# Where the split of the next weight chunk stands at the end of a sublayer: inside the second tile's layer norm, or ahead of the first tile's transposes

## The chip, the cores and the metric

The kernel runs on one core of one Trainium2 chip. The metric is device time in microseconds (us), of which the median over several runs counts.

## What is computed

Four post-norm layers over 256 frames of width 1024. Each layer has a token mixer (`lru` in layers 0 and 3, `rwkv` in layer 1, `attn` in layer 2), a cross-attention into 256 memory tokens (`cross`) and a squared-ReLU MLP (`mlp`): twelve sublayers, and each ends in a residual and a layer norm.

```python
for i in range(DEPTH):                       # 4
    y = mixer[i % 3](h)                      # lru, rwkv, attn
    h = _layer_norm(DEEPNORM_ALPHA * h + y, ln_g[i, 0], ln_b[i, 0])
    y = memory_cross_attention(h, mem, mx_w_q[i], mx_w_kv[i], mx_w_o[i])
    h = _layer_norm(DEEPNORM_ALPHA * h + y, ln_g[i, 1], ln_b[i, 1])
    y = squared_relu_mlp(h, mlp_w1[i], mlp_w2[i])
    h = _layer_norm(DEEPNORM_ALPHA * h + y, ln_g[i, 2], ln_b[i, 2])
```

## The kernel before

The 256 frames are two tiles of 128 rows, `h[0]` and `h[1]` (`h_91` and `h_92` in the lists of instructions below). Nothing is scheduled at run time: each engine executes its instructions in the order in which the program issues them, and that order is written by hand.

**Weights.** Class `Stream` brings all weights as a fixed sequence of chunks of 128 x 1024 f32. `_dma` issues a chunk's transfer on SP's queue into one of four `wraw` buffers. `_split` turns a landed chunk into a high part `whi` (a cast on ScalarE, ACT, line 455) and a low part `wlo` (a subtraction on VectorE, DVE, line 456), in one of seven pairs of buffers, and then issues the transfer of a later chunk. A product of two f32 matrices is three matmuls on TensorE (PE): `whi` with the high part of the other operand (line 273), `wlo` with it (274), `whi` with the low part (275). `done(c)` says that chunk c's last matmul has been issued, and splits on while buffers are free; `more()` splits one chunk more, into the pair of the chunk that was done last. Such a cast has to wait until PE has read that pair for the last time.

**The end of a sublayer.** The output projection runs tile 0, then tile 1 (`out_gemm`, in `mlp` its last block). After a tile's matmuls `resid` (lines 375, 380) adds them to `h` and takes the statistics, and `ln` (lines 387 to 401) is the layer norm: the small operations of lines 387 and 389, a power on GpSimd (POOL, line 390), two instructions of line 395 that need the mean alone, and two of line 401 that need POOL's result. `ln` calls `aside` between the power and line 395.

**The start of the next.** `next_ht` gives a function that transposes tile 0 of the new `h`: eight transposes on PE (line 352) into two PSUM tiles `tp`, out of which ACT casts the high part (line 355) and DVE subtracts the low part (line 356), both into `ht`. `mm_piece` calls it as `near` just before the last two rows' worth of weights of tile 1, so that PE has three matmuls to run behind the transposes:

```python
for k in range(kpc):
    if near and ci == n - 1 and k == kpc - 1:
        near()
```

The next sublayer's first product then runs tile 0, and the transposes of tile 1 stand in the same way ahead of its last three matmuls. Where the next sublayer is `rwkv`, `near` copies the transposed tile to `hf` (line 1134) and takes a shifted difference `xx` (line 1135) instead.

There are eleven such passages from one sublayer to the next. By what stands on DVE there, the ten that the diff touches are of four kinds: five ends of `out_gemm` with four chunks (every `cross`, and `attn`), two with six chunks in two parts (`lru`), two ends of `mlp` ahead of `attn` and `lru`, and one end of `mlp` ahead of `rwkv`. The end of `rwkv` keeps its order.

Of the kernel before, what the change touches and what calls it, by code (L numbers as in the profile page):

```python
# [29 lines left out]
G0 = 1  # L30
RES = 8
RESL = 2, 2, 2, 2
ASIDE = 1
LF = 18
LV = 0
GNP = 1
# [192 lines left out]
def _hl(hi, lo, p=128):  # L229
    return lambda kt: (hi[:p, kt, :], lo[:p, kt, :])  # L230


class Kern:
# [430 lines left out]
    def out_gemm(self, name, idx, n, lhs, p):  # L664

        for nh in range(2):
            a = [self.acc(), self.acc()]
            parts = [range(n)] if n <= 4 else [range(n // 2), range(n // 2, n)]
            for part in parts:
                end = part is parts[-1]  # L670
                ch = [self.st.take(name, (*idx, nh, q), p, 1024) for q in part]
                last = end and nh == 1
                near = self.next_ht() if last else None
                for t in range(2):
                    self.mm_piece(a[t], ch, lhs[t], p, 512, kt0=2 * part[0], start=part[0] == 0, stop=end,
                                  last=t == 1 and not last, near=near if t else None)
                    if last and t == 0:
                        self.st.more()
                    if end:
                        self.resid(t, nh, a[t])  # L680
                    if last:
                        self.ln_end(t, ch)

    def ln_end(self, t, ch):

        def aside():
            self.st.done(ch[0])
            self.st.more()

        self.ln(t, aside=aside if t and ASIDE else None)  # L690
        if t and not ASIDE:
            aside()
        if t:
            keep = DEFER if self.si < len(self.subs) and self.subs[self.si][0] != "rwkv" else 0
            for c in ch[1:len(ch) - keep]:
                self.st.done(c)
            self.owed = ch[len(ch) - keep:]
        if self.si >= len(self.subs):
            self.nc.sync.dma_start(self.out[t * 128:(t + 1) * 128, :], self.h[t])
        elif t:  # L700
            self.gb_due = 2
# [14 lines left out]
    def mlp(self, l):  # L716
        nc, tc = self.nc, self.tc
        NB = 8
        with tc.tile_pool(name="mlp", bufs=2, reuse_waits="tile") as p:
            accs = None  # L720
            sq, aT = [], {}

            def w1(b):
                hi = p.tile([128, 4, T], F32R, name="ahi", tag="ahi")
                lo = p.tile([128, 4, T], F32R, name="alo", tag="alo")
                ts = [slice(t * 128, (t + 1) * 128) for t in range(2)]
                for t in range(2):
                    aT[b, t] = _hl(hi[:, :, ts[t]], lo[:, :, ts[t]])
                if b:
                    for c, a, a2 in self.gemm_t("w1", (l, b), self.hT, (self.acc, self.acc) if b == 1 else (self.mm, self.tp)):  # L730
                        if c % 2 == 0:
                            r = p.tile([128, 2, T], F32, name="rel", tag="rel")
                        nc.scalar.copy(r[:, c % 2, :], a2)  # L733
                        nc.vector.tensor_tensor(out=r[:, c % 2, :], in0=a, in1=r[:, c % 2, :], op=ALU.add)  # L734
                        if c % 2:
                            sl = slice(c - 1, c + 1)
                            nc.vector.scalar_tensor_tensor(out=r, in0=r, scalar=0.0, in1=r, op0=ALU.max, op1=ALU.mult)  # L737
                            nc.scalar.copy(hi[:, sl, :], r)  # L738
                            nc.vector.tensor_tensor(out=lo[:, sl, :], in0=r, in1=hi[:, sl, :].bitcast(F32), op=ALU.subtract)
                            while sq:  # L740
                                self.to_hl(*sq.pop(0), 4)
                    return
                ch = self.chunks("w1", (l, b), 4, 128, 1024)
                for t in range(2):
                    a = self.mm()
                    self.mm_piece(a, ch, self.hT[t], 128, 512, last=t == 1, near=None if t else lambda: self.hT[1])
                    r = p.tile([128, 512], F32, name="rel", tag="rel")
                    nc.scalar.activation(r, a, AF.Relu)
                    nc.vector.tensor_tensor(out=r, in0=r, in1=r, op=ALU.mult)
                    sq.append((r, hi[:, :, ts[t]], lo[:, :, ts[t]]))  # L750

            for b in range(NB + 1):
                if b < NB:
                    w1(b)
                if b == 0:
                    continue
                if b == 1:
                    accs = [[self.acc() for _ in range(2)] for _ in range(2)]
                chs = [self.chunks("w2", (l, b - 1, nh), 2, 128, 1024) for nh in range(2)]
                near = self.next_ht() if b == NB else None  # L760
                for t in range(2):
                    for nh in range(2):
                        self.mm_piece(accs[t][nh], chs[nh], aT[b - 1, t], 128, 512, start=b == 1, stop=b == NB,
                                      last=t == 1 and b < NB, near=near if t and nh else None)
                        if b == NB:
                            if t == 0 and nh == 0:
                                self.st.more()
                            self.resid(t, nh, accs[t][nh])
                    if b == NB:
                        self.ln_end(t, chs[0] + chs[1])  # L770
                if b == 5 and self.coming("rwkv"):
                    self.rw_first()
# [365 lines left out]
    def rwkv(self, l, j):  # L1138
# [550 lines left out]
        oT, acc, ch = {}, [[None, None], [None, None]], [[], []]  # L1689
# [45 lines left out]
        self.mm_piece(acc[0][1], ch[1][3:], oT[0], 128, 512, kt0=6, start=False)  # L1735
        self.resid(0, 1, acc[0][1])
        near = self.next_ht()
        self.ln_end(0, ch[1])
        self.mm_piece(acc[1][1], ch[1], oT[1], 128, 512, near=near)
        self.resid(1, 1, acc[1][1])  # L1740
        self.ln_end(1, ch[1])
        r2.close()
        r1.close()
        return []
# [198 lines left out]
```

## Time and profile before

| | us |
|---|---|
| median of 3 runs | 1813.78 |
| lowest and highest of them | 1811.99, 1815.51 |
| profiled execution, its own time | 1802.43 |
| its span in the trace | 1800.6 |

The rows below are of the profiled execution. A time in them is counted from the start of the span. A DVE or ACT row merged as "x2" gives the first start and the time over both.

### The profile page before, as it was taken

To read this page: it belongs to the slowest core of one execution; us is meant where nothing else is said; L and a number is where in the kernel's file an instruction comes from. 1 tells how busy PE (TensorE), PEld (TensorE's weight loads), DVE (VectorE), ACT (ScalarE), POOL (GpSimd) and SP (SyncE) were. 2 spreads that over 40 slices of the span, in tenths; PEclk is the share of its full clock that TensorE was granted. 3 is DMA by queue.
4 is the path that set the end of the run, shared out by engine and by line. 5 is a ranking of instruction groups with operands and counts; after the bars stand their busy time and mean duration, and the time that the engine had idled before them with its cause. 6 is when DMAs were issued, how large, how long until landed. Compare 5 with 4: busy or idle time off the path is not lost.

```text
span 1800.6 us, 25667 instructions
## 1 busy us (share of the span) xinstructions
PE 1736.4 (96%) x10032; PEld 1453.8 (81%) x10032; DVE 1252.3 (70%) x1809; ACT 871.6 (48%) x1338; POOL 55.3 (3%) x64
## 2 busy tenths in 40 slices
PE   8999999999999989999999999999999999999998
PEld 7888988888777656888887888888888887988886
DVE  6587776667578798776667567776667587677665
ACT  6754534444543134544444544634444674545442
POOL 2000000000000001000000000000000000000000
PEclk9999999999999999999999999999999999999999
DMA  7464555555242224455555623545555545636552
GB/s 243 138 205 175 186 185 192 187 187 202 95 144 86 91 93 137 151 187 194 189 190 197 244 94 119 186 164 187 187 188 189 168 147 164 208 120 231 186 187 94
DMA packets 92927, 302.39 MB, mean 168 GB/s; under 512 B 11906, under 2 KB 19586, under 8 KB 92676
## 3 DMA queue, kind: packets, MB, share of 16 engines
q1 hardware_dynamic: 91780, 297.92, 49.3%
q10 hardware_dynamic: 1024, 2.81, 0.5%
q8 instruction: 79, 1.29, 0.3%
q14 instruction: 44, 0.36, 0.1%
HBM read 299.65 MB, written 1.05 MB: 167 GB/s over the span
## 4 chain that ended last, share of the span: by engine, by line
PE 78%; DVE 11%; ACT 4%; DMA 4%; issue 2%; POOL 0%; SPq 0%; DVEq 0%; ACTq 0%
PE acc L275 12%; PE acc L273 12%; PE acc L274 12%; PE tp L294 5%; PE mm L294 5%; PE acc L314 4%; PE acc L294 4%; PE acc L517 4%; PE tp L295 3%; PE mm L295 3%; DVE wlo L456 2%; PE acc L192 2%; PE mm L842 2%; PE tp L352 2%; PE acc L295 2%
## 5 line engine op out<-in xcount | busy, mean ns | idle before, releaser
L456 DVE TENSOR_TENSOR wlo<-wraw,whi 128x1024 fp32r<-128x1024 f32 (+3 forms) x505 | 593.7, 1206 | 133.3 <-ACT whi L455 121.9
L455 ACT CAST whi<-wraw 128x1024 fp32r<-128x1024 f32 (+3 forms) x505 | 507.2, 1039 | 163.5 <-PE acc L275 97.3
L273 PE MATMUL acc<-whi,ahi 128*128 128x512 f32 x512 | 200.3, 391 | 0.0
L275 PE MATMUL acc<-whi,alo 128*128 128x512 f32 x512 | 199.7, 390 | 0.0
L274 PE MATMUL acc<-wlo,ahi 128*128 128x512 f32 x512 | 199.4, 389 | 0.0
L273 PE MATMUL acc<-whi,ht 128*128 128x448 f32 (+1 forms) x368 | 142.4, 387 | 5.5 <-ACT whi L455 5.5
L274 PE MATMUL acc<-wlo,ht 128*128 128x448 f32 (+1 forms) x368 | 140.6, 382 | 3.5 <-DVE wlo L456 3.5
L275 PE MATMUL acc<-whi,ht 128*128 128x448 f32 (+1 forms) x368 | 140.4, 381 | 0.0
L294 PE MATMUL tp<-ht,whi 128*128 128x512 f32 x384 | 136.7, 398 | 0.0
L294 PE MATMUL mm<-ht,whi 128*128 128x512 f32 x384 | 136.5, 398 | 0.0
L294 PE MATMUL acc<-ht,whi 128*128 128x512 f32 x352 | 126.0, 400 | 1.9 <-DVE qkT L987 1.9
L275 PEld LDWEIGHTS acc<-whi,alo 128*128 128x128 f32 x512 | 96.1, 188 | 20.9
L273 PEld LDWEIGHTS acc<-whi,ahi 128*128 128x128 f32 x512 | 96.1, 188 | 20.2
L274 PEld LDWEIGHTS acc<-wlo,ahi 128*128 128x128 f32 x512 | 96.2, 188 | 19.2
L295 PE MATMUL tp<-ht,wlo 128*128 128x256 f32 x384 | 107.9, 281 | 0.0
L295 PE MATMUL mm<-ht,wlo 128*128 128x256 f32 x384 | 107.8, 281 | 0.0
L295 PE MATMUL acc<-ht,wlo 128*128 128x256 f32 x352 | 98.7, 280 | 0.0
L734 DVE TENSOR_TENSOR rel<-mm,rel 128x256 f32<-128x256 f32 x48 | 18.6, 425 | 110.4 <-ACT rel L733 110.4
L355 ACT CAST ht<-tp 128x512 fp32r<-128x512 f32 x40 | 22.8, 589 | 135.3 <-PE tp L352 134.3
L738 ACT CAST ahi<-rel 128x512 fp32r<-128x512 f32 x56 | 34.8, 622 | 110.0 <-DVE rel L737 110.0
L294 PEld LDWEIGHTS tp<-ht,whi 128*128 128x128 f32 x384 | 72.2, 188 | 18.0
L294 PEld LDWEIGHTS mm<-ht,whi 128*128 128x128 f32 x384 | 72.1, 188 | 17.6
(387 smaller groups left out, 3419.3 us busy)
## 6 DMA issues: line engine op xcount, KB each, us to landing
wraw<-in_w SPq DMA_DIRECT2D x256, 512.0 KB, 4.5
wraw<-in_w_kv SPq DMA_DIRECT2D x64, 512.0 KB, 4.3
wraw<-in_lru_in SPq DMA_DIRECT2D x47, 448.0 KB, 4.7
wraw<-in_w_q SPq DMA_DIRECT2D x32, 512.0 KB, 4.3
wraw<-in_w_co SPq DMA_DIRECT2D x32, 512.0 KB, 4.7
wraw<-in_ca_qkv SPq DMA_DIRECT2D x24, 512.0 KB, 4.5
wraw<-in_lru_out SPq DMA_DIRECT2D x24, 448.0 KB, 5.0
ln_gt<-in_ln_g SPq DMA_DIRECT2D x12, 512.0 KB, 6.1
```

What stands on the lines that cost most here:

```text
L192: return f(*a, **k)
L273: nc.tensor.matmul(acc[:, :w], lhsT=a, rhs=wh[:p, ws], start=s, stop=False)
L274: nc.tensor.matmul(acc[:, :w], lhsT=a, rhs=wl[:p, ws], start=False, stop=False)
L275: nc.tensor.matmul(acc[:, :w], lhsT=b, rhs=wh[:p, ws], start=False, stop=e)
L294: self.nc.tensor.matmul(four, lhsT=wh[:, ws], rhs=xy, start=s, stop=False)
L295: self.nc.tensor.matmul(four[:, :2], lhsT=wl[:, ws], rhs=x, start=False, stop=e)
L314: self.nc.tensor.matmul(a, lhsT=w[:, ws], rhs=v, start=s and i == 0, stop=e and i == 2)
L352: self.nc.tensor.transpose(dst_ps[:n, j * p:(j + 1) * p], s, self.ident[:p, :p])
L455: self.nc.scalar.copy(hi, src)
L456: self.nc.vector.tensor_tensor(out=lo, in0=src, in1=hi.bitcast(F32), op=ALU.subtract)
L517: nc.tensor.matmul(a, lhsT=u, rhs=w[:, ws], start=s, stop=e)
L842: nc.tensor.matmul(ps[:CT, gate * T:(gate + 1) * T], lhsT=gw[gate][:, n, :], rhs=xc[g][:, k, :], start=n == ks[0][0], stop=n == ks[-1][0])
```

## The change

At the ten ends, `done(ch[0])` and `more()` are called by `room`, ahead of `near`, and no longer by `aside` within the layer norm of tile 1. Each such call splits one chunk. The last layer norm of the kernel has no chunk left to split, before and after.

```diff
-                near = self.next_ht() if last else None
+                near = self.room(ch, self.next_ht()) if last else None
...
-    def ln_end(self, t, ch):
+    def room(self, ch, near):
+
+        def f():
+            self.st.done(ch[0])
+            self.st.more()
+            near()
+        return near and f
+
+    def ln_end(self, t, ch, roomy=True):
 
         def aside():
             self.st.done(ch[0])
             self.st.more()
 
-        self.ln(t, aside=aside if t and ASIDE else None)
-        if t and not ASIDE:
-            aside()
+        self.ln(t, aside=aside if t and not roomy else None)
...
-                near = self.next_ht() if b == NB else None
+                near = self.room(chs[0], self.next_ht()) if b == NB else None
...
-        self.ln_end(0, ch[1])
+        self.ln_end(0, ch[1], False)
...
-        self.ln_end(1, ch[1])
+        self.ln_end(1, ch[1], False)
```

The order of PE's, POOL's and SP's instructions stays as it is. In the changed kernel the lines behind the removed constant have a number lower by one (`wlo` is line 455, `whi` 454).

On DVE, at the end of layer 0's `cross` ahead of `mlp`: `wlo` is the split, `ht<-tp,ht` the low part of tile 0's transposes, `h_92` tile 1. Before:

```order
L401 SCALAR_TENSOR_TENSOR h_91<-h_91,rstd,ln_bt 128x512 x2
L356 TENSOR_TENSOR ht<-tp,ht 128x512 x2
L375 SCALAR_TENSOR_TENSOR h_92<-h_92,acc 128x512
L380 BN_STATS bnst<-h_92 128x6
L387 BN_AGGR bnmv<-bnst 128x2
L389 TENSOR_SCALAR rstd<-bnmv 128x1
L456 TENSOR_TENSOR wlo<-wraw,whi 128x1024
L395 SCALAR_TENSOR_TENSOR h_92<-h_92,bnmv,ln_gt 128x512 x2
L401 SCALAR_TENSOR_TENSOR h_92<-h_92,rstd,ln_bt 128x512 x2
```

After:

```order
L400 SCALAR_TENSOR_TENSOR h_91<-h_91,rstd,ln_bt 128x512 x2
L455 TENSOR_TENSOR wlo<-wraw,whi 128x1024
L355 TENSOR_TENSOR ht<-tp,ht 128x512 x2
L374 SCALAR_TENSOR_TENSOR h_92<-h_92,acc 128x512
L379 BN_STATS bnst<-h_92 128x6
L386 BN_AGGR bnmv<-bnst 128x2
L388 TENSOR_SCALAR rstd<-bnmv 128x1
L394 SCALAR_TENSOR_TENSOR h_92<-h_92,bnmv,ln_gt 128x512 x2
L400 SCALAR_TENSOR_TENSOR h_92<-h_92,rstd,ln_bt 128x512 x2
```

The split has moved from between `rstd` and the first scaling of `h_92` to between the last scaling of `h_91` and the subtraction for tile 0's `ht`. All else keeps its order.

On ACT, at the same place, `whi` is the cast of the split, `ht` the casts of tile 0 and then of tile 1. Before:

```order
L355 CAST P_2047<-mm 128x2x2x128 x2
L455 CAST whi<-wraw 128x1024 x5
L355 CAST ht<-tp 128x512 x2
L455 CAST whi<-wraw 128x1024 x2
L355 CAST ht<-tp 128x512 x2
L455 CAST whi<-wraw 128x1024
```

After:

```order
L354 CAST P_2047<-mm 128x2x2x128 x2
L454 CAST whi<-wraw 128x1024 x6
L354 CAST ht<-tp 128x512 x2
L454 CAST whi<-wraw 128x1024
L354 CAST ht<-tp 128x512 x2
L454 CAST whi<-wraw 128x1024
```

One cast has moved from behind tile 0's `ht` to ahead of it.

On DVE, at the end of layer 1's `mlp` ahead of `attn`. Before:

```order
L401 SCALAR_TENSOR_TENSOR h_91<-h_91,rstd,ln_bt 128x512 x2
L375 SCALAR_TENSOR_TENSOR h_92<-h_92,acc 128x512
L380 BN_STATS bnst<-h_92 128x6
L356 TENSOR_TENSOR ht<-tp,ht 128x512 x2
L375 SCALAR_TENSOR_TENSOR h_92<-h_92,acc 128x512
L380 BN_STATS bnst<-h_92 128x6
L387 BN_AGGR bnmv<-bnst 128x2
L389 TENSOR_SCALAR rstd<-bnmv 128x1
L456 TENSOR_TENSOR wlo<-wraw,whi 128x1024
L395 SCALAR_TENSOR_TENSOR h_92<-h_92,bnmv,ln_gt 128x512 x2
```

After:

```order
L400 SCALAR_TENSOR_TENSOR h_91<-h_91,rstd,ln_bt 128x512 x2
L374 SCALAR_TENSOR_TENSOR h_92<-h_92,acc 128x512
L379 BN_STATS bnst<-h_92 128x6
L455 TENSOR_TENSOR wlo<-wraw,whi 128x1024
L355 TENSOR_TENSOR ht<-tp,ht 128x512 x2
L374 SCALAR_TENSOR_TENSOR h_92<-h_92,acc 128x512
L379 BN_STATS bnst<-h_92 128x6
L386 BN_AGGR bnmv<-bnst 128x2
L388 TENSOR_SCALAR rstd<-bnmv 128x1
L394 SCALAR_TENSOR_TENSOR h_92<-h_92,bnmv,ln_gt 128x512 x2
```

Here the residual of half of tile 1 (`h_92`, `bnst`) stands ahead of tile 0's `ht` in both, and the split now comes between them.

## Rows read from the trace of the kernel before

**Rows 1.** The page: busy us, share of the span and instructions of each engine.
```profile
PE 1736.4 (96%) x10032; PEld 1453.8 (81%) x10032; DVE 1252.3 (70%) x1809; ACT 871.6 (48%) x1338; POOL 55.3 (3%) x64
```

**Rows 2.** Waits of PE over the span: us in total, times, longest.
```profile
PE tp L352 <- DVE h L401: 9.7, 10, 1.3
```

**Rows 3.** Timeline, DVE, `cross` to `mlp`, layer 0: start us, us, instruction [idle before].
```profile
245.04 1.41 DVE L401 SCALAR_TENSOR_TENSOR h<-h,rstd,ln_bt 128x512 f32<-128x512 f32 x2
...
247.78 1.29 DVE L356 TENSOR_TENSOR ht<-tp,ht 128x512 fp32r<-128x512 f32 x2 [1.32 <-ACT ht L355]
...
250.66 0.15 DVE L389 TENSOR_SCALAR rstd<-bnmv 128x1 f32<-128x1 f32 x1
250.74 1.23 DVE L456 TENSOR_TENSOR wlo<-wraw,whi 128x1024 fp32r<-128x1024 f32 x1
...
253.21 1.41 DVE L401 SCALAR_TENSOR_TENSOR h<-h,rstd,ln_bt 128x512 f32<-128x512 f32 x2
...
255.68 1.28 DVE L356 TENSOR_TENSOR ht<-tp,ht 128x512 fp32r<-128x512 f32 x2
```

**Rows 4.** Timeline, ACT, same end.
```profile
247.16 1.08 ACT L355 CAST ht<-tp 128x512 fp32r<-128x512 f32 x2 [8.85 <-PE tp L352]
```

**Rows 5.** Timeline, PE, same end, and layer 3's end of `cross`.
```profile
242.89 0.39 PE L275 MATMUL acc<-whi,ol 128*128 128x512 f32 x1
...
246.52 1.03 PE L352 MATMUL tp<-ident,h 128*128 128x128 f32 x8
...
254.10 1.29 PE L352 MATMUL tp<-ident,h 128*128 128x128 f32 x8 [0.96 <-DVE h L401]
...
256.41 0.50 PE L275 MATMUL mm<-whi,ht 128*128 128x512 f32 x1
...
1617.22 1.29 PE L352 MATMUL tp<-ident,h 128*128 128x128 f32 x8 [0.97 <-DVE h L401]
```

**Rows 6.** Instructions on tile `wraw` at the same end, 230 to 250 us.
```profile
L106 SPq DMA_DIRECT2D wraw<-in_w x5: 327/328/328, 233.6 to 239.9; - x5
...
DMA to landing us min/median/max: 4.6/4.8/5.0
```

**Rows 7.** Timeline, DVE then PE, `lru` to `cross`, layer 0.
```profile
150.85 1.41 DVE L401 SCALAR_TENSOR_TENSOR h<-h,rstd,ln_bt 128x512 f32<-128x512 f32 x2
...
152.98 1.40 DVE L356 TENSOR_TENSOR ht<-tp,ht 128x512 fp32r<-128x512 f32 x2 [0.72 <-ACT ht L355]
...
154.03 0.39 PE L275 MATMUL acc<-whi,ht 128*128 128x512 f32 x1
...
159.37 1.29 PE L352 MATMUL tp<-ident,h 128*128 128x128 f32 x8 [0.86 <-issue]
```

**Rows 8.** Timeline, DVE then PE, `mlp` to `attn`, layer 1.
```profile
954.25 1.29 DVE L356 TENSOR_TENSOR ht<-tp,ht 128x512 fp32r<-128x512 f32 x2
...
959.70 1.41 DVE L401 SCALAR_TENSOR_TENSOR h<-h,rstd,ln_bt 128x512 f32<-128x512 f32 x2
...
955.04 0.46 PE L275 MATMUL acc<-whi,ht 128*128 128x512 f32 x1
...
960.58 1.29 PE L352 MATMUL tp<-ident,h 128*128 128x128 f32 x8 [0.97 <-DVE h L401]
```

**Rows 9.** Timeline, DVE, `mlp` to `rwkv`; last row: chain that ended last.
```profile
428.72 0.70 DVE L380 BATCH_NORM_STATS2 bnst<-h 128x6 f32<-128x512 f32 x1
429.91 1.23 DVE L1135 TENSOR_TENSOR xx<-hf 128x1024 f32<-128x1024 f32 x1 [0.49 <-ACT hf L1134]
...
431.68 1.79 PE tp L1181 x16
```

**Rows 10.** Timeline, DVE, last layer norm of the kernel.
```profile
1794.08 0.15 DVE L389 TENSOR_SCALAR rstd<-bnmv 128x1 f32<-128x1 f32 x1
...
1795.47 1.41 DVE L401 SCALAR_TENSOR_TENSOR h<-h,rstd,ln_bt 128x512 f32<-128x512 f32 x2
```

**Rows 11.** Busy us of PE, PEld, DVE, ACT, POOL in a stretch inside `mlp`.
```profile
300.00:400.00 100.00, 100.00 (x504) 84.59 (x503) 62.85 (x73) 46.03 (x61) 0.00 (x0) 1.00 0.57 197
```

More of the change, by code (lines that the diff above doesn't have):

```diff
@@ L32 @@
 RESL = 2, 2, 2, 2
-ASIDE = 1
 LF = 18
```

## The prediction

> **What bounds the kernel.** I began with the page: PE is busy for 96% of the span [rows 1], so only what makes PE wait, or frees it from a wait, can move the end. I then read PE's waits. Their largest entry is this change's place: the transposes of tile 1 wait for line 401, the last operation of that tile's layer norm, 10 times and 9.7 us in all [rows 2]. One of the ten is the end of `rwkv`, which is not edited; the `lru` end of layer 0 has the same wait under the name "issue" [rows 7]. Last I went through DVE, ACT and PE in order of time at each of the ten edited ends, to see whether DVE has room where the split goes.
>
> At a `cross` end DVE works through tile 0's `ht`, tile 1's residual, the statistics, `rstd`, then the split (`wlo`), then lines 395 and 401, and PE stands still for 0.96 us until the first of line 401 is done [rows 3, 5]. The split lies on the chain that PE waits for. Ahead of tile 0's `ht`, in contrast, DVE idles for 1.32 us, because it needs PE's transposes and ACT's cast first [rows 3].
>
> **What taking it out of the layer norm gives.** From the start of `rstd` to the start of line 401 it is 253.21 - 250.66 = 2.55 us with the split between [rows 3]. The last layer norm of the kernel has none and takes 1795.47 - 1794.08 = 1.39 us [rows 10]; the changed order on DVE is that of this layer norm. So line 401 comes 2.55 - 1.39 = 1.16 us earlier after `rstd`. POOL's power, which runs at the same time, is in both figures. The same instruction on DVE costs as much wherever it is put; what decides is whether it fills idle time there.
>
> **Five ends with four chunks (`cross`, `attn`).** Line 401 of tile 0 ends at 245.04 + 1.41 = 246.45, and `ht` starts at 247.78 [rows 3]. The split takes 1.23 us [rows 3], so it ends near 247.7 and just fits. That needs the cast on ACT done by 246.45. ACT idles for 8.85 us up to 247.16 [rows 4], so it is free. The cast needs the chunk's transfer: five are issued between 233.6 and 239.9 and land some 4.8 us later, at most 5.0 [rows 6]; even the last of them, a later chunk, is there by 244.9. It also needs PE to be done with chunk `ch[0]`, whose last matmul for tile 1 closes the second of eight groups of three; it ends at 242.89 + 0.39 = 243.28 [rows 5]. The cast should run from about 243.4 to 244.5, and both halves of the split are hidden, the one by ACT's idle time and the other by DVE's. If the cover were missing, this end would look like those of `mlp` below.
>
> Line 401 then starts at 253.21 - 1.16 = 252.05, and what released the transposes at 254.10 does so at 252.94. PE is ready at about 254.10 - 0.96 = 253.14, so its wait is gone. Behind the transposes PE needs tile 1's low part of `ht`, which DVE started at 255.68, behind another split that follows line 401 without a pause, and the matmul with it started at 256.41 [rows 3, 5]. This is again DVE's chain, 1.16 us earlier. I take 1.16 for each of the five. The lower bound is nothing (if the split does not fit). The upper one is 0.96 plus the 0.26 that the eight transposes lose because the second line 401 comes late (1.29 us here, against 1.03 for tile 0's, which wait for nothing [rows 5]), about 1.2. Layer 3 has the same wait, 0.97 [rows 5], and so have the three between. Sum: 5 x 1.16 = 5.8 us.
>
> **Two ends of `lru`.** The gap ahead of `ht` is only 0.72 us here [rows 7]. One split occupies DVE for 1.15 us, from its start at 250.74 until the next instruction could start; I get it as 2.55 - 1.39, rounded. It starts as line 401 ends, 152.2, and `ht` starts near 153.32 instead of 152.98: 0.34 late. From the start of `ht` to the first matmul with a low part it is 0.79 us where PE waits for it (954.25 to 955.04 [rows 8]), so that matmul comes at 154.11 instead of 154.03 [rows 7]: PE loses 0.08. Tile 1's line 401 comes 1.16 - 0.34 = 0.82 earlier, and PE, which waited 0.86 for it [rows 7], follows by as much. 0.8 us each, between 0 and 0.86. Sum: 1.6 us.
>
> **Two ends of `mlp` ahead of `attn` and `lru`.** Here tile 0's `ht` starts on DVE at 954.25 with no idle time before it [rows 8]: half of tile 1's residual and statistics already fill the gap. The split in front delays `ht` by 1.15, and the matmul at 955.04, which waits for it, with it [rows 8]. The rest of DVE's chain is the same work in another order, so line 401 stays near 959.70, and the transposes near 960.58: PE's wait of 0.97 there [rows 8] turns into a wait of 1.15 at the low part. I count 0, between a loss of 0.2 and a gain of 0.3 each.
>
> **One end of `mlp` ahead of `rwkv`.** DVE idles 0.49 us ahead of `xx` [rows 9]. With the split there from 429.4, `xx` ends near 431.7 instead of 429.91 + 1.23 = 431.14, and PE's matmuls on it start at 431.68 [rows 9]. I count a loss of 0.1, at most 0.3. PE does not wait for line 401 here.
>
> **Queues.** SP's queue keeps its order; a transfer that waits for the split's buffer is issued some 4 us sooner (the split starts at 246.4, not 250.74), which only helps. POOL's order is unchanged.
>
> **A rule against the change.** ACT idles up to 247.16 and its next instruction is `ht` [rows 4]: whatever is put ahead of it stands between PE's transposes and PE's next product. The Trainium skill says that ScalarE and VectorE take their queue strictly in order (TensorE: Matmul & The Clock Gate, section "Architectural detail: the array is 16× 32×32, not 1× 128×128"); by that rule a cast that waits for its chunk holds up `ht` although its input is there. The idle time on ACT, with later work waiting behind `ht`, agrees. If the cast's inputs come as I read them, the sum is the same; if not, the rule gives the slower rival below.
>
> **Sum.** 5.8 + 1.6 + 0 - 0.1 = 7.3 us. The profiled execution took 1802.43 us and would take 1795.1. The median of the runs is 11 us above it, 0.6%; I take the 7.3 us off the median: 1813.78 - 7.3 = 1806.5. Does it stay? Inside `mlp` PE is busy for all of 100 us [rows 11], so no transfer paces the stretches behind `cross`, and a shift at their start reaches their end.
>
> **Rivals.**
> - *The split does not fit.* If at the five ends DVE cannot take it up at 246.4, or lost more than the 0.1 us that is spare, `ht` moves as in `mlp`: PE waits about 1.15 us for the low part and no longer for line 401. Each end gains about 0.1, and the two of `lru` still 0.8, so about 2 us in all: 1811.7, no change that can be told. For it: the spare time is a tenth of a us. Against it: a slip of 0.3 us still leaves 0.8 of the 1.16.
> - *The gain is given back.* A later wait that does not move with PE, such as a transfer, takes the time: 1813.8. Against it: full PE in `mlp` [rows 11], and transfers whose issue hangs on buffers that come free with PE.
> - *Slower: the cast is late.* If the cast were released only with tile 1's last matmul, say 1.1 us after ACT's `ht` of today, at 248.3, it would end at 249.4, and DVE's `ht`, behind the split, would start at 250.5 instead of 247.78. PE would lose some 2.6 us at tile 0, and get back the wait of 0.96 and little more at tile 1: about 1.5 us lost at each of ten ends, 1813.8 + 15 = 1829. It decides once the cast starts later than about 246.1 (247.16 less its 1.05); my reading has it ready 2.7 us before.
>
> **How the numbers follow.** I call the forecast 0.73, the split not fitting 0.15, the gain given back 0.05, the late cast 0.07. About 0.2% (3.6 us) is what a measurement of this kernel can tell from no change. The forecast's own range is 1803.5 to 1809.5 (5.8 and 1.6 by their bounds, 9.1 at most with 0.6 of `mlp`, and half of the runs' spread of 3.5 us). The stated range reaches to the case in which the split does not fit: 1803 to 1812. Faster: 0.73, and 0.04 of the second case: 0.77. No change 0.16, slower 0.07.
>
> **What would show it.** After the change, at the `cross` ends: no DVE idle time ahead of `ht` and `ht` still 0.6 us behind ACT's first cast; `rstd` to line 401 at 1.39 us; the entry "tp <- h line 401" down from 9.7 by the 4.8 of the five ends or more. At the `mlp` ends: a wait of about 1.1 us of line 275 for `ht`. POOL's power shorter. I am wrong if the transposes of tile 0 are followed by longer waits at the five ends, or if the cast waits on PE with `ht` behind it, or if a later stretch grows by what these ends lose.

## The result, and the profile after

The changed kernel took 1803.6 us (median of 11 runs, 1801.95 to 1814.37), the kernel before 1813.8 in 11 runs beside it (1809.22 to 1824.32): a ratio of 0.9948, with a 95% interval of 0.9926 to 0.9971, or 9.4 us less (5 to 13). The prediction was 1806.5, with 1803 to 1812 as its range, and faster with a chance of 0.77.

The two profiled executions must not be compared by their ends. That of the changed kernel is 5.1 us longer (span 1805.7 against 1800.6), though the kernel is faster. The page after has PE no less busy than [rows 1]:

```profile
PE 1742.7 (97%) x10032; PEld 1459.8 (81%) x10032; DVE 1252.2 (69%) x1809; ACT 872.7 (48%) x1338; POOL 50.3 (3%) x64
```

The ten ends below are 7.6 us shorter in it, so 12.7 us were lost elsewhere. 8.9 of them lie ahead of the first end, where the two kernels run the same instructions; the rest lies in `cross` of layer 1 (1.4), `attn` (1.5) and `lru` of layer 3 (0.8). These are the windows from the start to tile 0's transposes at the first `lru` end, of the kernel before and then of the changed one (busy time and count for each engine, granted clock, share of DMA, GB/s):

```profile
0.00:151.69 151.69, 138.31 (x685) 119.51 (x686) 102.10 (x140) 93.74 (x145) 12.34 (x31) 0.99 0.62 198
```

```profile
0.00:160.56 160.56, 142.48 (x685) 122.89 (x686) 102.09 (x140) 94.91 (x146) 12.17 (x31) 0.97 0.61 187
```

They took 8.9 us longer, at a granted clock of 0.97 instead of 0.99. So the change is read from intervals: at each end, from the start of tile 0's transposes to the first matmul behind tile 1's transposes.

| end | before | after | difference, each | predicted |
|---|---|---|---|---|
| four chunks: `cross` of layers 0 to 3, `attn` | 8.63 (all) | 7.47, 7.48 | -1.16 | -1.16 |
| `lru`, layers 0 and 3 | 8.73, 8.72 | 7.78 | -0.95 | -0.8 |
| `mlp` to `attn`, `mlp` to `lru` | 8.63, 8.49 | 8.52, 8.37 | -0.11, -0.12 | 0 |
| `mlp` to `rwkv` | 9.99 | 10.31 | +0.32 | +0.1 |
| sum of the ten | | | -7.6 | -7.3 |

PE's waits after, to be set beside [rows 2]:

```profile
PE tp L351 <- DVE h L400: 2.0, 3, 1.1
...
PE acc L274 <- DVE ht L355: 1.6, 2, 0.8
```

The wait of the transposes for the layer norm has gone from 9.7 us in ten places to 2.0 in three, of which 1.1 is the end of `rwkv` that the diff leaves alone, 0.6 a wait of tile 0 at the end of `lru` in layer 3 that was there before, and 0.3 the end of `mlp` ahead of `lru`. A new wait, for the low part of `ht`, has come in two places: the `mlp` ends.

The first `cross` end after, by DVE, then ACT, then PE, in order of time (answers to [rows 3 to 5]):

```profile
252.97 1.41 DVE L400 SCALAR_TENSOR_TENSOR h<-h,rstd,ln_bt 128x512 f32<-128x512 f32 x2
...
254.30 1.22 DVE L455 TENSOR_TENSOR wlo<-wraw,whi 128x1024 fp32r<-128x1024 f32 x1
...
255.70 1.29 DVE L355 TENSOR_TENSOR ht<-tp,ht 128x512 fp32r<-128x512 f32 x2 [0.19 <-ACT ht L354]
...
258.59 0.15 DVE L388 TENSOR_SCALAR rstd<-bnmv 128x1 f32<-128x1 f32 x1
...
259.98 1.41 DVE L400 SCALAR_TENSOR_TENSOR h<-h,rstd,ln_bt 128x512 f32<-128x512 f32 x2
...
262.44 1.28 DVE L355 TENSOR_TENSOR ht<-tp,ht 128x512 fp32r<-128x512 f32 x2
...
251.25 1.06 ACT L454 CAST whi<-wraw 128x1024 fp32r<-128x1024 f32 x1 [4.99 <-PE acc L274]
...
255.09 1.07 ACT L354 CAST ht<-tp 128x512 fp32r<-128x512 f32 x2 [2.78 <-PE tp L351]
...
254.45 1.03 PE L351 MATMUL tp<-ident,h 128*128 128x128 f32 x8
...
260.91 1.25 PE L351 MATMUL tp<-ident,h 128*128 128x128 f32 x8
...
261.92 0.48 PE L272 MATMUL mm<-whi,ht 128*128 128x512 f32 x1
...
263.18 0.50 PE L274 MATMUL mm<-whi,ht 128*128 128x512 f32 x1
```

The cast starts at 251.25, released by PE (line 274, `ch[0]`'s last matmul), and ends almost 3 us before ACT's first `ht`. The split follows line 400 on DVE without a pause, and 0.19 us of DVE's idle time are left ahead of `ht`, of 1.32 before. From `rstd` to line 400 it is 259.98 - 258.59 = 1.39 us, the figure of [rows 10]. The transposes of tile 1 have no wait in brackets any more; `ht` follows 2.46 us behind line 400, as it followed line 401 by 2.47 in [rows 3].

### The profile page after: what moved, and what is told of

It reads as the page before. It is cut to its first block, busy times and chain, and to the rows that moved or that the text cites. A ratio compares the mean times of both kernels' runs of the same rounds, so it can differ in the third digit from the quotient of the medians.

```text
span 1805.7 us, 25667 instructions
## 1 busy us (share of the span) xinstructions
PE 1742.7 (97%) x10032; PEld 1459.8 (81%) x10032; DVE 1252.2 (69%) x1809; ACT 872.7 (48%) x1338; POOL 50.3 (3%) x64
## 3 DMA queue, kind: packets, MB, share of 16 engines
q10 hardware_dynamic: 1024, 2.81, 0.6%
q8 instruction: 79, 1.29, 0.3%
## 4 chain that ended last, share of the span: by engine, by line
PE 80%; DVE 9%; DMA 5%; ACT 4%; issue 2%; SPq 1%; POOL 0%; DVEq 0%; ACTq 0%
PE acc L274 12%; PE acc L272 12%; PE acc L273 12%; PE tp L293 5%; PE mm L293 5%; PE acc L293 4%; PE acc L516 4%; PE acc L313 4%; PE tp L294 3%; PE mm L294 3%; PE mm L847 2%; PE acc L191 2%; PE tp L351 2%; DMA wraw<-in_lru_in 2%; PE acc L294 2%; DVE wlo L455 2%
## 5 line engine op out<-in xcount | busy, mean ns | idle before, releaser
L272 PEld LDWEIGHTS acc<-whi,ht 128*128 128x128 f32 x368 | 70.2, 191 | 16.9 <-ACT whi L454 5.9
```

Source lines behind the costliest of these rows:

```text
L272: nc.tensor.matmul(acc[:, :w], lhsT=a, rhs=wh[:p, ws], start=s, stop=False)
```

## The experiments

A timed kernel ran 12 times (the one with the split behind the layer norm 6 times) beside the kernel before, to which its ratio is given with a 95% interval. The lengths of the ends are those of the table above, read from one trace each.

**The ends apart.** The split goes ahead only at the four-chunk ends:

```diff
-                near = self.room(ch, self.next_ht()) if last else None
+                near = (self.room(ch, self.next_ht()) if n <= 4 else self.next_ht()) if last else None
...
-                near = self.room(chs[0], self.next_ht()) if b == NB else None
+                near = self.next_ht() if b == NB else None
```

(the other ends keep `aside`). Expected: 

> Only the five ends with four chunks have the split ahead of tile 0's transposes; the other five keep it in the layer norm. My theory (the split costs nothing only where it fills DVE's idle time): from tile 0's transposes to the matmul behind tile 1's, 8.63 us before, these five take 7.47 and the others are as before; 5 x 1.16 = 5.8 us less than before, a ratio near 0.997. Rival (a shorter layer norm is worth the same at every end): half of the 7.5 us that the full change gave in its trace, 3.8 us, with about 0.75 at each of the five.

Measured: 0.9964 (0.9950 to 0.9978), 6.5 us less; 7.47 or 7.48 at the five, and at the others the values of the kernel before. The reverse, with `n > 4` and `room` kept in `mlp`: 

> Only the two ends of lru and the three of mlp have the split ahead; the five with four chunks keep it in the layer norm. My theory: lru 2 x 0.95 less, mlp ahead of attn and lru 2 x 0.1 less, mlp ahead of rwkv 0.3 more: 1.8 us less than before, a ratio near 0.999, not to be told from no change. At the mlp ends PE waits some 0.8 us for the low part of ht instead of line 401. Rival (same worth at every end): 3.8 us less, 0.998.

Measured: 0.9988 (0.9973 to 1.0002), 2.2 us less. 8.63 at the five, 7.78 at `lru`, 8.51 and 8.38 at `mlp`, 10.30 ahead of `rwkv`. The same wait in this kernel is the five ends' 0.96 and what was left after:

```profile
PE tp L351 <- DVE h L400: 6.8, 8, 1.1
```

With the split ahead at all but the three `mlp` ends: 

> The split ahead at the five ends with four chunks and the two of lru; the three mlp ends keep it in the layer norm. My theory: 5.8 + 1.9 = 7.7 us less than before, a ratio near 0.996, within 0.3 us of the full change; the mlp ends read as before (wait of 1 us for line 401, none for ht). Rival (same worth at every end): 7 of 10 of the gain, 5.3 us.

Measured: 0.9959 (0.9944 to 0.9975), 7.4 us less; the `mlp` ends read 9.99, 8.62 and 8.49 as before. So a shorter layer norm is not worth the same everywhere. The gain is that of the five and, less, of the `lru` ends, and the two parts add up: by the ends 5.8 + 1.8 = 7.6, as in the change; by the runs 6.5 + 2.2 = 8.7 against 9.4, each known to 2.5 to 4 us.

**Another place outside the layer norm.** The kernel before, with `aside()` called behind the layer norm:

```diff
-ASIDE = 1
+ASIDE = 0
```

> The split stands behind tile 1's layer norm instead of within it, at all eleven ends. My theory: line 401 comes 1.16 us earlier as in the change, but the split is of the fourth chunk of the next first product, which PE reaches some 4 us behind tile 0's transposes; the split would end near 254.6 in the times of the first cross end, PE would wait for wlo about 2 us there, before tile 1's transposes, and each end would be about 1 us longer than before: 8 to 10 us more, a ratio near 1.005. Rival (leaving the layer norm is what counts, whatever the place): about 7 us less, 0.996.

Measured: 1.0063 (1.0044 to 1.0081), 11 us more. The first `cross` end, DVE and then PE:

```profile
259.02 1.41 DVE L401 SCALAR_TENSOR_TENSOR h<-h,rstd,ln_bt 128x512 f32<-128x512 f32 x2
...
260.35 2.35 DVE L456 TENSOR_TENSOR wlo<-wraw,whi 128x1024 fp32r<-128x1024 f32 x2
...
261.62 0.50 PE L274 MATMUL mm<-wlo,ht 128*128 128x512 f32 x1 [1.96 <-DVE wlo L456]
```

The same wait at the end of `rwkv`, which the change does not touch and this version does:

```profile
720.75 0.79 PE L274 MATMUL acc<-wlo,ht 128*128 128x512 f32 x1 [3.28 <-DVE wlo L456]
```

Line 401 does come early, 1.39 us behind `rstd`, but the two splits behind it end at 262.7, and PE, which has come to the chunk of the first, stands still 1.96 us for its `wlo`. The interval is 9.5 to 10.3 us at the four-chunk ends, 9.99 and 9.29 at `mlp` ahead of `attn` and `lru`, and 12.35 instead of 9.86 at the end of `rwkv`. At the two `lru` ends, where the next product has its four chunks already, it is 7.56: 0.2 less than in the change, where I had expected about 1 us more than before. The rival is refuted: leaving the layer norm is not what counts, but where the split goes, and who waits for its result.

**Is the idle time what pays?** Four small subtractions on DVE ahead of tile 0's `ht`, at the four `cross` ends, first in the kernel before (split in the layer norm), then in the changed one:

```diff
+    def padded(self, near):
+        def f():
+            with self.tc.tile_pool(name="pad", bufs=1, side="right") as p:
+                pad = p.tile([128, 240], F32, name="pad")
+                for i in range(4):
+                    x = self.h[0][:, 240 * i:240 * i + 240]
+                    self.nc.vector.tensor_tensor(out=pad, in0=x, in1=x, op=ALU.subtract)
+            near()
+        return near and f
```

> The kernel before, with the split within the layer norm, and at the four cross ends four small subtractions (128 x 240, of h with itself into a pad that nothing reads) on DVE ahead of tile 0's ht; they add work of about one split, some 1.2 to 1.4 us. My theory (DVE has 1.32 us of idle time there): from tile 0's transposes to the matmul behind tile 1's stays 8.63 us, or grows by the 0.1 or 0.2 by which the filler is longer than the gap. Rival (work ahead of ht holds it up by its own length): 9.8 us or more. The attn end, without the filler, stays at 8.63.

> The changed kernel with the same filler behind the split, ahead of tile 0's ht, at the four cross ends. My theory (the split has filled the gap): the filler counts in full, the interval grows from 7.47 to 8.6 or 8.8 us, with a wait of PE for the low part of ht of 0.8 to 1.1 us that the changed kernel does not have there; the attn end stays at 7.47. Rival (there is still room ahead of ht, the gain came from elsewhere): 7.5 to 7.7 us.

One profiled run each. In the kernel before, DVE:

```profile
253.97 1.73 DVE L691 TENSOR_TENSOR pad<-h 128x240 f32<-128x240 f32 x4
...
255.62 1.28 DVE L356 TENSOR_TENSOR ht<-tp,ht 128x512 fp32r<-128x512 f32 x2
```

In the changed kernel, DVE and then PE:

```profile
248.36 1.22 DVE L455 TENSOR_TENSOR wlo<-wraw,whi 128x1024 fp32r<-128x1024 f32 x1
...
249.50 1.73 DVE L698 TENSOR_TENSOR pad<-h 128x240 f32<-128x240 f32 x4
...
251.15 1.28 DVE L355 TENSOR_TENSOR ht<-tp,ht 128x512 fp32r<-128x512 f32 x2
...
251.88 0.50 PE L274 MATMUL mm<-whi,ht 128*128 128x512 f32 x1 [1.17 <-DVE ht L355]
```

The filler is longer than I had meant: DVE's next instruction starts 1.65 us behind its start. In the kernel before it costs 0.23 us of that (8.86 instead of 8.63), in the changed kernel 1.37 (8.84 instead of 7.47), with a wait of PE for the low part of 1.17. Both lengths are a little above the forecast, and both rivals (9.8 us or more; 7.5 to 7.7 us) are refuted. So the gap took about 1.4 us for nothing, once, and the split has used it up. `attn`, without filler, read 8.63 and 7.48.

**A better version.** From the table I put the split by the kind of end, and put off one more chunk's split, which stands ahead of tile 1's `ht` on DVE (`DEFER = 2`); at the `lru` ends all of it goes behind tile 1's `ht`. 

> The split is put by the kind of end: ahead of tile 0's transposes at the five ends with four chunks and at the mlp ends ahead of attn and lru, behind tile 1's ht at the two lru ends (there the next product has four chunks ready), in the layer norm at mlp ahead of rwkv; and one more chunk's split goes behind tile 1's ht everywhere (DEFER 2). My theory: intervals of 7.2 to 7.4 us at the four-chunk ends (7.47 in the change), 7.3 to 7.5 at lru (7.78), 8.2 to 8.4 at the two mlp ends (8.52), 10.0 at mlp ahead of rwkv (10.3): 2 us less than the change, 9 to 10 us less than before, a ratio near 0.995. Rival (the chunk put off is missed by PE): new waits for wlo or whi of a us or two per end, no faster than the change.

Measured: 0.9995 (0.9980 to 1.0009), although the ends read 7.48, 7.57, 8.51, 8.37 and 10.0, 8.3 us less than before in sum: as forecast ahead of `rwkv`, 0.1 above the forecast at `lru`, and no better than the change elsewhere. At a four-chunk end the forecast had no room to come true: in the change tile 1's transposes already follow PE's work without a wait, and only the 0.2 us by which the eight of them take longer than tile 0's was left to gain. What the ends gained, the stretches between them lost. Two kernels took the two edits apart: the version by place with `DEFER` left at 1, and the change with this edit alone:

```diff
-DEFER = 1
+DEFER = 2
```

> As the version that puts the split by place, but with one chunk put off as in the kernel before (DEFER 1). My theory (the second chunk put off is what cost that version its gain, by longer waits at the starts of attn, rwkv and lru and a lower granted clock behind them): intervals of 7.47 us at the four-chunk ends, 7.57 at lru, 8.5 at mlp ahead of attn and lru, 10.0 at mlp ahead of rwkv; 5.8 + 2.3 + 0.2 = 8.3 us less than before, a ratio near 0.9955, about that of the change or a little under it. Rival (the split behind tile 1's ht at the lru ends, or the mlp ends, cost it): a ratio near 0.9995 again.

> The changed kernel with DEFER 2 in place of 1, nothing else. My theory: the ends read as in the change, but the stretches behind them grow: a longer wait for qkT at the start of attn (3 to 4 us where the change has 2.3) and a granted clock under 1 there; the ratio goes from 0.995 to about 0.999. Rival (putting off a second chunk is harmless): 0.995 or less.

Measured: by place with `DEFER` 1, 0.9963 (0.9948 to 0.9978); the change with `DEFER` 2, 0.9986 (0.9972 to 1.0001). Against the change's 0.9948 the second chunk put off costs some 7 us (2 to 12 by the two intervals), and in the version by place some 6 (0.9995 against 0.9963, 2 to 10); these pairs were not timed beside each other. The placement alone is not told apart from the change. Where the time goes, a trace each does not settle. The longer wait for `qkT` that I forecast at the start of `attn` is there, 3.2 us against 2.3 in the change, but it is 3.1 in the kernel of the other ends, which puts off one chunk; the granted clock of that stretch is 0.99 with one and with two. The windows of the stretches `rwkv` and `cross` of layer 2, with `DEFER` 2 and then in the change:

```profile
440.54:708.97 268.43, 248.08 (x2213) 182.10 (x2214) 202.17 (x423) 97.28 (x156) 16.38 (x9) 0.98 0.32 109
...
1128.19:1196.16 67.97, 66.35 (x356) 57.18 (x355) 50.70 (x76) 38.14 (x66) 0.92 (x1) 0.97 0.48 163
```

```profile
445.20:710.25 265.05, 245.07 (x2213) 181.57 (x2214) 202.19 (x423) 97.21 (x156) 16.37 (x9) 0.99 0.33 110
...
1131.00:1197.10 66.10, 64.83 (x355) 55.62 (x354) 49.99 (x76) 36.97 (x65) 0.92 (x1) 1.00 0.50 168
```

They are 3.4 and 1.9 us longer, with PE busy longer for the same matmuls at a lower granted clock. But such stretches differ by as much between kernels that put off one chunk: `rwkv` took 267.8 us and `cross` of layer 2 67.6 in the trace with the split at the four-chunk ends only, `rwkv` 265.1 in that without the `mlp` ends. What a late chunk has to do with the clock stays open. By its ends the version by place with `DEFER` 1 would be 0.7 us ahead of the change, which these runs cannot tell; none of the versions is shown to be faster than the change.

**The `mlp` ends.** As the version by place, with the subtraction of the two `mlp` ends on POOL:

```diff
-        self.nc.vector.tensor_tensor(out=lo, in0=src, in1=hi.bitcast(F32), op=ALU.subtract)
+        (getattr(self, 'lo_eng', None) or self.nc.vector).tensor_tensor(out=lo, in0=src, in1=hi.bitcast(F32), op=ALU.subtract)
```

> As the version that puts the split by place, but at the mlp ends ahead of attn and lru the subtraction of the moved split runs on POOL instead of DVE. My theory (these ends are bound by the sum of DVE's work from tile 0's residual to tile 1's line 401, so only less of it helps): the interval there falls by up to 1.15 us, to about 7.2 us, and the wait for the low part of ht goes, provided that POOL is done before the power of tile 1's layer norm, some 5 us after the cast. Rival: POOL takes longer than that, or holds DVE up while it runs, and the interval is 8.5 us or more.

One profiled run. The interval is 7.96 us at both ends, instead of 8.51 and 8.37, and the wait for `ht` is gone, but PE now waits 1.38 and 1.11 us for tile 0's layer norm, ahead of the interval: from tile 0's power to the matmul behind tile 1's transposes it is 12.07 us instead of 11.08 at the end of layer 1, and 11.80 instead of 10.94 at that of layer 2. DVE, then POOL, at the end of layer 1:

```profile
961.88 3.53 DVE L400 SCALAR_TENSOR_TENSOR h<-h,rstd,ln_bt 128x512 f32<-128x512 f32 x2
...
960.79 0.92 POOL L389 TENSOR_TENSOR rstd<-rstd,mhalf 128x1 f32<-128x1 f32 x1 [172.37 <-DVE rstd L388]
...
961.68 2.52 POOL L455 TENSOR_TENSOR wlo<-wraw,whi 128x1024 fp32r<-128x1024 f32 x1
```

POOL's subtraction takes 2.52 us, and the two of line 400, which run at the same time, 3.53 instead of 1.41. The rival's mechanism holds: POOL holds DVE up, and the ends are 0.9 and 1 us worse, though the loss lies ahead of the interval, where I had looked for it within.

## Why the prediction held, step by step

**The terms.** The price of the split in the layer norm, 1.16 us, is what the five ends gained, each. That it fits ahead of `ht` was right with 0.19 us to spare. That tile 1's low part of `ht` follows DVE's chain, and not PE, was right too: the matmul with it starts 263.18 - 254.45 = 8.73 us behind tile 0's transposes, before 256.41 - 246.52 = 9.89 [rows 5], so 1.16 earlier, not more.

Two readings were wrong and did no harm. Of the ten waits of [rows 2] one is not tile 1's but that of tile 0's transposes at the end of `lru` in layer 3, which start at 1514.82 after a wait of 0.61 us. And the upper bounds behind the range add up to some 6.1 + 1.7 + 0.6 = 8.4 us, not 9.1; its end of 1803.5 agrees with 8.4.

**`lru`.** I counted 0.8 and it was 0.95. Before, DVE:

```profile
152.98 1.40 DVE L356 TENSOR_TENSOR ht<-tp,ht 128x512 fp32r<-128x512 f32 x2 [0.72 <-ACT ht L355]
154.30 0.68 DVE L375 SCALAR_TENSOR_TENSOR h<-h,acc 128x512 f32<-128x512 f32 x1
```

After, DVE and then PE:

```profile
161.04 1.22 DVE L455 TENSOR_TENSOR wlo<-wraw,whi 128x1024 fp32r<-128x1024 f32 x1
...
162.18 1.28 DVE L355 TENSOR_TENSOR ht<-tp,ht 128x512 fp32r<-128x512 f32 x2
163.38 0.68 DVE L374 SCALAR_TENSOR_TENSOR h<-h,acc 128x512 f32<-128x512 f32 x1
...
166.45 1.41 DVE L400 SCALAR_TENSOR_TENSOR h<-h,rstd,ln_bt 128x512 f32<-128x512 f32 x2
...
167.36 1.23 PE L351 MATMUL tp<-ident,h 128*128 128x128 f32 x8
...
168.34 0.48 PE L272 MATMUL acc<-whi,ht 128*128 128x512 f32 x1
```

The split did delay `ht`, by what I counted: it starts 162.18 - 160.56 = 1.62 us behind tile 0's transposes, before 152.98 - 151.69 = 1.29, so 0.33 later (I said 0.34). What I left out is that `ht` itself gets shorter. Before, its two subtractions took 1.40 us, and DVE's next instruction started 154.30 - 152.98 = 1.32 behind the first; begun later, they took 1.28, and the next instruction started 1.20 behind. That gives 0.12 back. Tile 1's layer norm is 1.16 shorter as in the other ends, and 0.33 - 0.12 - 1.16 = -0.95. Line 400 to the matmul behind the transposes is 1.89 us, as before (158.53 to 160.42).

**`mlp` ahead of `attn`.** DVE, then PE, to be set beside [rows 8]:

```profile
961.54 1.21 DVE L455 TENSOR_TENSOR wlo<-wraw,whi 128x1024 fp32r<-128x1024 f32 x1
...
962.66 1.28 DVE L355 TENSOR_TENSOR ht<-tp,ht 128x512 fp32r<-128x512 f32 x2
...
966.93 1.41 DVE L400 SCALAR_TENSOR_TENSOR h<-h,rstd,ln_bt 128x512 f32<-128x512 f32 x2
...
963.40 0.50 PE L274 MATMUL acc<-whi,ht 128*128 128x512 f32 x1 [0.83 <-DVE ht L355]
...
967.84 1.28 PE L351 MATMUL tp<-ident,h 128*128 128x128 f32 x8
```

`ht` starts as soon as the split lets it, PE waits 0.83 us for its low part (I said about 1.1; the matmul with it starts 1.00 later behind tile 0's transposes than before) and no longer for line 400. The chain of DVE's work is the bound, and only its order changed: 0.1 us.

**`mlp` ahead of `rwkv`.** This term was too small. I had PE's matmuls on `xx` 0.1 us late by the end of `xx`; they come 0.3 late. Before, PE's weight loads for them:

```profile
431.41 1.87 PEld L1181 LDWEIGHTS tp<-xx,lora1x 128*128 128x128 f32 x16
```

After, DVE and then PE's weight loads:

```profile
436.07 1.21 DVE L455 TENSOR_TENSOR wlo<-wraw,whi 128x1024 fp32r<-128x1024 f32 x1
...
437.19 1.22 DVE L1140 TENSOR_TENSOR xx<-hf 128x1024 f32<-128x1024 f32 x1
...
438.46 1.86 PEld L1186 LDWEIGHTS tp<-xx,lora1x 128*128 128x128 f32 x16 [0.24 <-DVE xx L1140]
```

`xx` starts behind the split, as predicted, and the weight loads of the matmuls on it wait for its end, 0.24 us as the row counts it. I had taken 431.68 of [rows 9], from the chain that ended last, for the start of PE's work on `xx`; the loads, which take `xx` in, had started at 431.41. From tile 0's transposes to these loads it is 431.41 - 428.16 = 3.25 us before and 438.46 - 434.89 = 3.57 after. The loss of 0.32 is just over the bound of 0.3 that I gave.

**What was not in the sum.** The misses partly cancel (`lru` 0.3 more, `mlp` ahead of `attn` and `lru` 0.2 more, `mlp` ahead of `rwkv` 0.2 less); that the sum of 7.3 comes so near to the 7.6 of the ends is in part luck. The ends give 7.6 us and the runs 9.4, with 7.6 inside their interval; the rest is not settled, and with it the median came out 2.9 us below the 1806.5, near the low end of the range. That the shift at an end reaches the end of the next stretch was right: the stretch of each `mlp` from a `cross` end to its own transposes took 173.0 us before and after.

**The rivals.** The split fitted. Nothing is seen to be given back: `cross` of layer 1 and `attn`, longer in the trace after, read 57.2 to 59.8 and 152.8 to 155.5 us in kernels whose program is the same there, and the runs gained more than the ends. The cast was not late: it started 3.8 us ahead of ACT's first `ht`. How late it may come was not tried.

## What to carry to other kernels

Work on an engine that others wait for costs nothing only where that engine itself waits: find its idle time just ahead of an instruction that waits for another engine, compare its length with the work, and ask who needs the moved work's result and when. Do this for every place that an edit touches: one edit made five places 1.16 us better, two 0.95, left two nearly alone (0.1) and made one 0.3 worse. Where executions differ by more than the edit is worth, compare intervals between two fixed instructions, not spans.

## What the runs showed of the hardware

- Executions of the same instructions differ by stretch: up to the first transposes 151.7 us in one trace and 160.6 in another, at granted clocks of 0.99 and 0.97 (1 is the level of 2.4 GHz), and `rwkv`, where PE is busy for 245 of 265 us, 265.0 to 269.7 over eight kernels, while the stretches of the first three `mlp`, where PE hardly waits [rows 11], repeat to 0.1 us in 173.0.
- A subtraction of 128 x 1024 f32 on POOL took 2.52 us, against 1.22 on DVE, and held up DVE's instructions with two operands in SBUF that started 0.2 us behind it (3.53 us instead of 1.41 for the two of line 400). The Trainium skill says that POOL and DVE share a pair of ports to SBUF, which one of them holds for a whole instruction while the other stands still, and counts a DVE operation with two SBUF inputs among those concerned when POOL's instruction reads SBUF, as this one does (SBUF — State Buffer, section "SBUF: two separate sides"); these rows agree.
- POOL's power at tile 1 of the first `cross` end took 1.48 us while the split ran beside it on DVE, and 0.98 at the same end after the change.
